# Value projections and the last projection by token, with 512 weight columns a product

## The chip, the cores and the metric

The kernel runs on one core of a Trainium2 chip. The metric is the device time of one execution in microseconds. Its time before is 1223.8 us, the median of three runs (1220.79 to 1223.92).

## The reference

Two blocks of a transformer-like network follow each other on 256 tokens of width 1024, in float32. The parts that the change touches are the value projections and the last projection:

```python
# first block, layer 0: retention mixer
a_val, a_gate, q, k, v, g = jnp.split(h @ w_in, splits, axis=-1)
# second block
(gq, gk, gv, gg, ga1, fq, fk, fv, ff, mq, bg) = jnp.split(h @ w_in[l], IN_OFFSETS, axis=-1)
mk, mv = jnp.split(_rmsnorm_2(mem, g_mem[l]) @ w_mem_kv[l], 2, axis=-1)
x = x + merged @ w_out[l]
h2 = _rmsnorm_2(x, g_ffn[l])
x = x + (jax.nn.silu(h2 @ w_ffn_gate[l]) * (h2 @ w_ffn_up[l])) @ w_ffn_down[l]
```

The values v, gv, fv and mv have 512 columns each. The last projection has 2816 rows of weights and 1024 columns.

## The kernel before

The residual x lies in SBUF by channel: 128 partitions, 8 blocks of 128 channels, 256 tokens (`x`, 128 x 8 x 256). Every operand of a dense product is split into a high and a low part of type F32R, and `mm3` (lines 319 to 321) adds three products: high x high, high x low and low x high. Weights come in pieces of 1 MB or less: `load` sends them over SP's queue into one of four buffers, `split` makes the high part on ACT (L314) and the low part on DVE (L315), four chunks a piece, into one of two buffers.

`lin` takes 128 x 128 blocks of the weights as the stationary operand and 256 tokens of the activation as the moving one; its result lies by channel. `lin_tok` does the reverse for the values, which are wanted by token: 128 x 128 blocks of the activation are stationary, and 256 columns of the weights move. A value projection is two pieces of 256 columns, in the mixer of the first block (L567), for the memory (`tok` at L1238), and twice in the second block (gv at L1347, fv at L1430). Their results go to two PSUM banks of the tag "mm"; ACT copies them out, scaled per token in `tok`.

`memory` is a generator whose steps are put between other work: one for the norm, one for each half of the keys, one for each half of the values. `memat` (1, 3, 0) says how many are taken behind the S5 layer, how many ahead of the second feed-forward stage, and how many behind it; what is left is drained behind it (L1676, L1677).

The last stage is `swiglu` (L1517). `up(q)` makes the hidden activations of part q, of 4, 4 and 3 pairs of weight pieces (L1539 to L1542 on DVE, L1540 on ACT); `down(q)` multiplies them by their rows of `w_down` into four PSUM banks of the tag "at", by channel, with `lin`. The order is up(0), up(1), down(0), up(2), down(1), down(2). In the last `down`, each bank's result is scaled per token (L1552), added to x (L1553) and sent out by channel.

The order of instructions on each engine, and on SP's queue, is not the order of the source. A planner puts it down once, from its own estimates of durations and from the order in which the source states the work: of what is ready, the earlier stated goes first. Each queue then runs strictly in that order, so a transfer that waits holds everything behind it on SP.

Of the kernel before, what the change touches and what calls it, by code (L numbers as in the profile page):

```python
# [7 lines left out]
F32 = mybir.dt.float32  # L8
# [3 lines left out]
AF = mybir.ActivationFunctionType  # L12
ALU = mybir.AluOpType
MT = bass.MemoryType
T = 256
# [14 lines left out]
def layout(v):  # L30
# [41 lines left out]
    d["w_down"] = dense(f(v["w_ffn_down_2"])[0])  # L72
# [102 lines left out]
class K:  # L175
# [155 lines left out]
    def lin_tok(self, ps, W, act):  # L331

        for k in range(8):
            for c in range(2):
                s = slice(c * 128, c * 128 + 128)
                self.mm3(ps[:, c], act[0][:, k, s], act[1][:, k, s], W[0][:, k], W[1][:, k],
                         k == 0 and c == 0, k == 7 and c == 1)
# [163 lines left out]
    def mixer0(self, x, h, fill, need, after_conv, each):  # L501
        nc = self.nc
# [62 lines left out]
        for j in range(2):  # L565
            ps = self.pair()
            self.lin_tok(ps, step_piece("w_in", 8 + j), h)  # L567
            nc.scalar.copy(v[:, :, 256 * j:256 * j + 256], ps)
# [595 lines left out]
    def tok(self, dst, name, js, h, rc):  # L1164

        for n, j in enumerate(js):
            ps = self.pair()
            self.lin_tok(ps, self.piece(name, j), h)
            for b in range(2):
                self.nc.scalar.activation(dst[:, b, 256 * n:256 * n + 256], ps[:, b], AF.Copy, scale=rc[:, b:b + 1])  # L1170
# [49 lines left out]
    def memory(self):  # L1220
# [16 lines left out]
        for n in range(2):  # L1237
            self.tok(self.mv[:, :, 256 * n:256 * n + 256], "w_mkv", (2 + n,), (hh, hl), rc)  # L1238
            yield
# [29 lines left out]
    def block2(self, x, h, rc, rb, each):  # L1269
# [77 lines left out]
        self.tok(gv, "w_in2", (2, 3), h, rc)  # L1347
# [82 lines left out]
        self.tok(fv, "w_in2", (10, 11), h, rc)  # L1430
# [86 lines left out]
    def swiglu(self, x, h, rb):  # L1517
# [4 lines left out]
        acc = [self.pair("at") for _ in range(4)]  # L1522
        hid = {}
        parts = ((0, 4), (4, 4), (8, 3))
        bc = rb[:, None, :].to_broadcast([128, 2, T])
        rh = self.keep([128, T], "rh")
        v.tensor_scalar_mul(rh, rb, 0.5)
        bch = rh[:, None, :].to_broadcast([128, 2, T])
# [16 lines left out]
        def down(q):  # L1545
            j0, nj = parts[q]
            for j in range(4):
                self.lin(acc[j], self.piece("w_down", j, 2 * j0, 2 * nj), hid[q], [(k, k) for k in range(2 * nj)], start=q == 0, stop=q == 2)
                if q == 2:
                    s = slice(2 * j, 2 * j + 2)  # L1550
# [6 lines left out]
        for q in range(3):  # L1557
            if q < 2:
                up(q + 1)
            down(q)  # L1560
# [156 lines left out]
```

## Time and profile before

| | us |
|---|---|
| median of three runs | 1223.8 |
| lowest and highest | 1220.79, 1223.92 |
| the profiled execution | 1223.6 |
| its span, first to last instruction | 1221.8 |

| engine | busy us | share of the span |
|---|---|---|
| PE (products) | 1164.1 | 95% |
| DVE | 888.7 | 73% |
| ACT | 610.9 | 50% |
| POOL | 96.8 | 8% |

The profile is one execution. A product's record lasts from its start to the end of its last column, and products overlap, so the distance from start to start is what counts. The DMA engines move 219 GB/s on average. The granted clock is TensorE's, as a share of 2.4 GHz; it is 0.979 over the span.

### The profile page before, as it was taken

How to read it: one execution, taken by the hardware profiler on the slowest of the kernel's cores; microseconds unless marked ns; L12 is line 12 of the kernel's file. 1: busy time of each engine (PE TensorE's matmuls, PEld its weight loads, DVE VectorE, ACT ScalarE, POOL GpSimd, SP SyncE). 2: the span in 40 equal slices, each digit the busy share in tenths (PEclk: the TensorE clock that was granted, in tenths of full speed). 3: DMA queues.
4: the chain of work that ended last, by engine and by line, in shares of the span. 5: the costliest groups of instructions: out<-in, count | busy, mean ns of one | idle time of the engine just before them, and what ended most of it. 6: DMA issues, size and time to landing. Idle time of an engine off the chain costs nothing. (4 is left out here: it accounts for less than half of the span.)

```text
span 1221.8 us, 25406 instructions
## 1 busy us (share of the span) xinstructions
PE 1164.1 (95%) x10482; PEld 1106.0 (91%) x10482; DVE 888.7 (73%) x1827; ACT 610.9 (50%) x1202; POOL 96.8 (8%) x132
## 2 busy tenths in 40 slices
PE   5899898999999966899999999999999999999998
PEld 3698688999999954899999999999999999999998
DVE  7879988988988869757666556676666676665564
ACT  3577345555555441646444445563465535544441
POOL 0077310000000015000000000000000000000000
PEclk9799998999999988999999999999999999999999
DMA  9888785688987999554565654452444454555541
GB/s 343 326 317 322 293 325 200 229 311 267 323 299 261 300 254 319 193 175 167 197 224 208 219 196 165 153 189 74 173 139 142 170 173 157 189 173 181 195 152 61
DMA packets 69979, 267.29 MB, mean 219 GB/s; under 512 B 7380, under 2 KB 35428, under 8 KB 43240
## 3 DMA queue, kind: packets, MB, share of 16 engines
q1 hardware_dynamic: 69864, 265.68, 63.4%
q8 instruction: 82, 1.34, 0.4%
q14 instruction: 33, 0.27, 0.1%
HBM read 246.85 MB, written 18.81 MB: 217 GB/s over the span
## 5 line engine op out<-in xcount | busy, mean ns | idle before, releaser
L315 DVE TENSOR_TENSOR lo<-w,hi 128x512 fp32r<-128x512 f32 (+1 forms) x640 | 422.5, 704 | 145.1 <-ACT hi L314 144.6
L314 ACT ACTIVATE hi<-w 128x512 fp32r<-128x512 f32 (+1 forms) x640 | 358.0, 625 | 325.4 <-PE mm L320 123.3
L319 PE MATMUL mm<-h,hi 128*128 128x256 f32 x1328 | 382.4, 288 | 1.3 <-ACT hi L314 0.8
L321 PE MATMUL mm<-h,lo 128*128 128x256 f32 x1328 | 380.4, 287 | 0.1
L320 PE MATMUL mm<-h,hi 128*128 128x256 f32 x1328 | 379.7, 286 | 0.2 <-DVE h L384 0.2
L319 PEld LDWEIGHTS mm<-h,hi 128*128 128x128 f32 x1328 | 257.0, 194 | 9.1 <-issue 3.6
L321 PEld LDWEIGHTS mm<-h,lo 128*128 128x128 f32 x1328 | 256.9, 194 | 2.7 <-issue 1.3
L320 PEld LDWEIGHTS mm<-h,hi 128*128 128x128 f32 x1328 | 256.9, 194 | 1.3 <-issue 0.7
L320 PE MATMUL at<-s,hi 128*128 128x256 f32 x720 | 204.4, 284 | 0.0
L319 PE MATMUL at<-s,hi 128*128 128x256 f32 x720 | 204.4, 284 | 0.0
L321 PE MATMUL at<-s,lo 128*128 128x256 f32 x720 | 203.9, 284 | 0.0
L319 PEld LDWEIGHTS at<-s,hi 128*128 128x128 f32 x720 | 138.0, 192 | 1.8 <-issue 1.4
L320 PEld LDWEIGHTS at<-s,hi 128*128 128x128 f32 x720 | 138.0, 192 | 0.6 <-issue 0.6
L321 PEld LDWEIGHTS at<-s,lo 128*128 128x128 f32 x720 | 137.8, 192 | 0.4 <-issue 0.4
L443 PE MATMUL fa<-wa,crep 128*32 128x256 f32 x704 | 52.9, 418 | 7.7 <-DMA wa<-in_ada_dram 3.5
L541 POOL TENSOR_TENSOR s<-s,cv 128x256 f32<-128x256 f32 x60 | 50.1, 872 | 39.5 <-ACT cv L540 39.4
L443 PEld LDWEIGHTS fa<-wa,crep 128*32 128x32 f32 x704 | 20.8, 116 | 26.8 <-DMA wa<-in_ada_dram 5.4
L319 PE MATMUL fp<-h,hi 128*128 128x256 f32 x144 | 41.1, 286 | 1.5 <-ACT hi L314 1.5
L320 PE MATMUL fp<-h,hi 128*128 128x256 f32 x144 | 40.9, 284 | 0.0
L321 PE MATMUL fp<-h,lo 128*128 128x256 f32 x144 | 40.7, 283 | 0.0
L540 ACT ACTIVATE cv<-ap,s 128x256 f32<-128x256 f32 x60 | 29.5, 506 | 17.3 <-POOL s L541 16.5
L937 ACT COPY Wt<-fp 128x512 f32<-128x512 f32 x32 | 18.6, 582 | 35.2 <-PE fp L936 28.5
(438 smaller groups left out, 1809.7 us busy)
## 6 DMA issues: line engine op xcount, KB each, us to landing
w<-in_fc_dram SPq DMA_DIRECT2D x64, 1024.0 KB, 5.0
wa<-in_ada_dram SPq DMA_DIRECT2D x44, 1024.0 KB, 6.1
w<-in_w_in_dram SPq DMA_DIRECT2D x38, 1024.0 KB, 4.9
w<-in_w_gate_dram SPq DMA_DIRECT2D x11, 1024.0 KB, 4.9
w<-in_w_up_dram SPq DMA_DIRECT2D x11, 1024.0 KB, 4.8
Vd<-V SPq DMA_DIRECT2D x16, 512.0 KB, 5.5
w<-in_w_out_dram SPq DMA_DIRECT2D x8, 1024.0 KB, 5.5
Wd<-Wt SPq DMA_DIRECT2D x16, 512.0 KB, 6.0
```

What stands on the lines that cost most here:

```text
L314: self.nc.scalar.activation(hi, h, AF.Copy)
L315: self.nc.vector.tensor_tensor(lo, h, hi.bitcast(F32), op=ALU.subtract)
L319: mm(ps, sh, mh, start=start, stop=False, skip_group_check=True)
L320: mm(ps, sh, ml, start=False, stop=False, skip_group_check=True)
L321: mm(ps, sl, mh, start=False, stop=stop, skip_group_check=True)
L443: nc.tensor.matmul(ps[32 * q:32 * q + 32], self.crep[:, 2 * k + k2], w[:, n:n + 256], start=k == 0 and k2 == 0, stop=k == 3 and k2 == 1, t ...
L540: nc.scalar.mul(t, src, w)
L541: nc.gpsimd.tensor_tensor(acc[:, ch], acc[:, ch], t, op=ALU.add)
L937: nc.scalar.copy(W[:, :, k], pt.rearrange("p (e x) -> p e x", e=4))
```

## The change

The value projections and the last projection get weights laid out in pieces of 512 columns (`w_v`, which holds the four value weights one after another, and `w_down`). `lin_tok` now multiplies 512 moving columns at once, for one half of the tokens and then the other, into two whole PSUM banks of the tag "at". A piece holds 4 row blocks by 512 columns in place of 8 by 256. `tok` evicts 512 columns at once. The memory's two value steps become one.

In `swiglu` the last projection's result now lies by token. For the sum the residual is wanted by token too: `turned` turns each of its eight blocks in squares of 32 on DVE (`v.transpose`), and 32 transfers on SP's queue put the squares where they belong; it is stated behind up(0). The final scaling and addition are one operation on DVE, in place, and the output leaves by token: four transfers of 256 KB, as before. The scale per token is kept as a column (`rt`) in place of a row (`rh`). In the last part the pieces of `w_down` have 4 and 2 row blocks.

```diff
--- before.py
+++ after.py
@@ -69,7 +69,9 @@
     d["w_out2"] = dense(f(v["w_out_2"])[0])
     d["w_gate"] = dense(f(v["w_ffn_gate_2"])[0])
     d["w_up"] = dense(f(v["w_ffn_up_2"])[0])
-    d["w_down"] = dense(f(v["w_ffn_down_2"])[0])
+    d["w_down"] = dense(f(v["w_ffn_down_2"])[0], 512)
+    w2v = lambda a: w2[:, a:a + 512]
+    d["w_v"] = con(np.concatenate([dense(a, 512) for a in (f(v["w_in"])[0][:, 2048:2560], w2v(512), w2v(2576), f(v["w_mem_kv_2"])[0][:, 512:])]))
 
     gp = lambda a: f(a)[0].reshape(2, 4, 16, 64).transpose(0, 3, 2, 1).reshape(128, 64)
     d["lam_re"], d["lam_im"] = con(gp(v["s5_lam_re"])), con(gp(v["s5_lam_im"]))
@@ -328,13 +330,20 @@
                 self.mm3(ps[:, ci], W[0][:, k, s], W[1][:, k, s], act[0][:, ka], act[1][:, ka],
                          start and n == 0 and ci == 0, stop and n == len(ks) - 1 and ci == len(cols) - 1)
 
-    def lin_tok(self, ps, W, act):
-
-        for k in range(8):
-            for c in range(2):
-                s = slice(c * 128, c * 128 + 128)
-                self.mm3(ps[:, c], act[0][:, k, s], act[1][:, k, s], W[0][:, k], W[1][:, k],
-                         k == 0 and c == 0, k == 7 and c == 1)
+    def lin_tok(self, ps, W, act, ks, start, stop):
+
+        for b in range(2):
+            s = slice(b * 128, b * 128 + 128)
+            for n, (k, ka) in enumerate(ks):
+                self.mm3(ps[b], act[0][:, ka, s], act[1][:, ka, s], W[0][:, k], W[1][:, k],
+                         start and n == 0, stop and n == len(ks) - 1)
+
+    def values(self, i, act, piece=None):
+
+        ps = [self.ps("at") for _ in range(2)]
+        for k0 in (0, 4):
+            self.lin_tok(ps, (piece or self.piece)("w_v", i, k0, 4, 512), act, [(k, k0 + k) for k in range(4)], k0 == 0, k0 == 4)
+        return ps
 
 
     def rsqrt(self, v, out=None):
@@ -562,10 +571,8 @@
             qk.append(dst)
         q, k = qk
         v = self.sb([128, 2, 512])
-        for j in range(2):
-            ps = self.pair()
-            self.lin_tok(ps, step_piece("w_in", 8 + j), h)
-            nc.scalar.copy(v[:, :, 256 * j:256 * j + 256], ps)
+        for b, ps in enumerate(self.values(0, h, step_piece)):
+            nc.scalar.copy(v[:, b], ps)
         rh, rl, ah, al = (self.sb([128, 4, T], F32R) for _ in range(4))
         os, ms = [], []
         for j in range(2):
@@ -1161,13 +1168,10 @@
         return u
 
 
-    def tok(self, dst, name, js, h, rc):
-
-        for n, j in enumerate(js):
-            ps = self.pair()
-            self.lin_tok(ps, self.piece(name, j), h)
-            for b in range(2):
-                self.nc.scalar.activation(dst[:, b, 256 * n:256 * n + 256], ps[:, b], AF.Copy, scale=rc[:, b:b + 1])
+    def tok(self, dst, i, h, rc):
+
+        for b, ps in enumerate(self.values(i, h)):
+            self.nc.scalar.activation(dst[:, b], ps, AF.Copy, scale=rc[:, b:b + 1])
 
     def heads(self, dst, name, js, h, g, rc, out=None):
 
@@ -1234,9 +1238,8 @@
         for n in range(2):
             self.heads(self.mk[:, 2 * n:2 * n + 2], "w_mkv", (n,), (hh, hl), self.col("g_mem_k"), rc)
             yield
-        for n in range(2):
-            self.tok(self.mv[:, :, 256 * n:256 * n + 256], "w_mkv", (2 + n,), (hh, hl), rc)
-            yield
+        self.tok(self.mv, 3, (hh, hl), rc)
+        yield
 
     def norm2_begin(self, x):
 
@@ -1344,7 +1347,7 @@
         self.mark("b2.gla")
 
         gv = self.sb([128, 2, 512])
-        self.tok(gv, "w_in2", (2, 3), h, rc)
+        self.tok(gv, 1, h, rc)
         gs = self.sb([128, 4, T])
         for c in range(2):
             pg = self.pair()
@@ -1427,7 +1430,7 @@
                     v.scalar_tensor_tensor(A[:, hd, o:o + nk], pn[:, 256 * a:256 * a + nk], cq[:, b, hd:hd + 1], causal[:, T - nk:], op0=ALU.add, op1=ALU.add)
         self.heads(fq, "w_in2", (6, 7), h, gq[:, 0:1], rc, rq[:, 0:4])
         self.heads(fk, "w_in2", (8, 9), h, self.col("g_fox_k"), rc)
-        self.tok(fv, "w_in2", (10, 11), h, rc)
+        self.tok(fv, 2, h, rc)
 
         def fox(hd, po):
             pl = self.ps()
@@ -1514,18 +1517,26 @@
             v.scalar_tensor_tensor(x[:, 2 * j:2 * j + 2], ps, 0.5, x[:, 2 * j:2 * j + 2], op0=ALU.mult, op1=ALU.add)
             each(j)
 
-    def swiglu(self, x, h, rb):
+    def swiglu(self, x, h, rb, rt):
 
         nc, v = self.nc, self.nc.vector
         tt = v.tensor_tensor
         K8 = [(k, k) for k in range(8)]
-        acc = [self.pair("at") for _ in range(4)]
         hid = {}
         parts = ((0, 4), (4, 4), (8, 3))
+        acc = [[self.ps("at") for _ in range(2)] for _ in range(2)]
+
+        xt, xb = self.sb([128, 2, 1024], tag="xt"), self.sb([128, 8, T], tag="xt")
+
+        def turned():
+            for k in range(8):
+                v.transpose(xb[:, k], x[:, k])
+            for i in range(4):
+                for j in range(4):
+                    for b in range(2):
+                        nc.sync.dma_start(xt[32 * j:32 * j + 32, b].rearrange("p (k i s) -> p k i s", k=8, i=4)[:, :, i],
+                                          xb[32 * i:32 * i + 32, :, 128 * b + 32 * j:128 * b + 32 * j + 32])
         bc = rb[:, None, :].to_broadcast([128, 2, T])
-        rh = self.keep([128, T], "rh")
-        v.tensor_scalar_mul(rh, rb, 0.5)
-        bch = rh[:, None, :].to_broadcast([128, 2, T])
 
         def up(q):
             j0, nj = parts[q]
@@ -1544,16 +1555,19 @@
 
         def down(q):
             j0, nj = parts[q]
-            for j in range(4):
-                self.lin(acc[j], self.piece("w_down", j, 2 * j0, 2 * nj), hid[q], [(k, k) for k in range(2 * nj)], start=q == 0, stop=q == 2)
+            for m in range(2):
+                for k0 in range(0, 2 * nj, 4):
+                    kn = min(4, 2 * nj - k0)
+                    self.lin_tok(acc[m], self.piece("w_down", m, 2 * j0 + k0, kn, 512), hid[q], [(k, k0 + k) for k in range(kn)],
+                                 q == 0 and k0 == 0, q == 2 and k0 + kn == 2 * nj)
                 if q == 2:
-                    s = slice(2 * j, 2 * j + 2)
-                    t = self.sb([128, 2, T])
-                    tt(t, acc[j], bch, op=ALU.mult)
-                    tt(x[:, s], t, x[:, s], op=ALU.add)
-                    nc.sync.dma_start(self.out[:, s], x[:, s])
+                    for b in range(2):
+                        o = xt[:, b, 512 * m:512 * m + 512]
+                        v.scalar_tensor_tensor(o, acc[m][b], rt[:, b:b + 1], o, op0=ALU.mult, op1=ALU.add)
+                        nc.sync.dma_start(self.out[:, b, 512 * m:512 * m + 512], o)
 
         up(0)
+        turned()
         for q in range(3):
             if q < 2:
                 up(q + 1)
@@ -1692,12 +1706,15 @@
 
                 self.block2(x, made[0][0], rc, rb, each)
             mem_pools.close()
-            with self.phase(s8=4):
+            with self.phase(s8=4, xt=2):
                 self.mark("norm2f")
                 rb = self.keep([128, T], "rb2")
-                nc.scalar.copy(rb, self.rms(x, st))
+                r = self.rsqrt_eps(self.sumsq(x, st)[:, :, 0])
+                nc.scalar.copy(rb, self.spread(r))
+                rt = self.keep([128, 2], "rt")
+                nc.vector.tensor_scalar_mul(rt, r, 0.5)
                 self.mark("swiglu")
-                self.swiglu(x, out[0][0], rb)
+                self.swiglu(x, out[0][0], rb, rt)
 
 
 def kernel(**inputs):
@@ -1708,9 +1725,9 @@
     nc = bacc.Bacc("TRN2", target_bir_lowering=False, num_devices=1)
     arrays = {f"in_{n}_dram": a for n, a in layout(inputs).items()}
     I = {n[3:-5]: nc.dram_tensor(n, a.shape, mybir.dt.from_np(a.dtype), kind="ExternalInput").ap() for n, a in arrays.items()}
-    out = nc.dram_tensor("out_0_dram", (128, 8, T), F32, kind="ExternalOutput").ap()
+    out = nc.dram_tensor("out_0_dram", (128, 2, 1024), F32, kind="ExternalOutput").ap()
     with tile.TileContext(nc, schedule_with_timeline_sim=True) as tc:
         K(tc, I, out, None).build()
     r = run_bass_kernel_spmd(nc, [arrays], core_ids=[0])
     got = r.results[0]["out_0_dram"]
-    return np.ascontiguousarray(got.transpose(2, 1, 0).reshape(1, T, 1024))
+    return np.ascontiguousarray(got.transpose(1, 0, 2).reshape(1, T, 1024))
```

## Rows read from the trace of the kernel before

**Rows 1.** The page, part 1: PE's busy time, share of the span, instructions.

```profile
PE 1164.1 (95%) x10482; PEld 1106.0 (91%) x10482; DVE 888.7 (73%) x1827; ACT 610.9 (50%) x1202; POOL 96.8 (8%) x132
```

**Rows 2.** By stage: busy us (count) PE PEld DVE ACT POOL, clock, DMA.

```profile
100.00:200.00 100.00, 92.90 (x865) 79.05 (x864) 89.14 (x197) 49.49 (x103) 34.85 (x34) 0.97 0.82 301
430.00:500.00 70.00, 44.17 (x738) 34.10 (x738) 54.99 (x104) 26.54 (x47) 24.71 (x38) 0.81 0.95 269
500.00:762.00 262.00, 262.00 (x2193) 261.95 (x2192) 167.71 (x328) 132.39 (x251) 2.87 (x3) 1.00 0.56 197
762.00:1024.00 262.00, 262.00 (x2118) 256.88 (x2116) 180.79 (x432) 138.14 (x281) 0.00 (x0) 0.99 0.45 152
1024.00:1177.00 153.00, 152.71 (x1271) 152.31 (x1271) 96.16 (x168) 72.37 (x136) 0.00 (x0) 1.00 0.53 178
```

**Rows 3.** Timeline of PE in the last projection: start us, us, line, tiles, shape.

```profile
1192.53 0.28 PE L320 MATMUL at<-s,hi 128*128 128x256 f32 x1
1192.65 0.28 PE L321 MATMUL at<-s,lo 128*128 128x256 f32 x1
```

**Rows 4.** Stretch around 45 us: its granted clock, and PE's timeline there.

```profile
44.00:47.00 3.00, 3.00 (x16) 3.00 (x16) 3.00 (x7) 1.31 (x3) 0.00 (x0) 0.50 0.87 311
44.20 0.41 PE L319 MATMUL mm<-h,hi 128*128 128x256 f32 x1
...
45.27 0.41 PE L321 MATMUL mm<-h,lo 128*128 128x256 f32 x1
```

**Rows 5.** PE's timeline near 763 and 940 us, and L1486 by form.

```profile
763.26 0.95 PE L167 MATMUL fa<-nw,q 128*128 128x2 f32 x8
...
764.27 0.28 PE L320 MATMUL mm<-lo,mhh 128*128 128x256 f32 x1
...
768.27 0.28 PE L321 MATMUL mm<-hi,mhl 128*128 128x256 f32 x1
...
939.74 1.02 PE L1486 MATMUL at<-s,mv 128*128 128x256 f32 x4
L1486 PE MATMUL at<-s,mv 128*128 128x256 f32 x16 | 4.1, 378 | 0.0
```

**Rows 6.** Groups by form: line, engine, operation, shape, count, busy us, mean ns.

```profile
L448 DVE STREAM_TRANSPOSE s<-fa 128x256 f32<-128x256 f32 x11 | 4.9, 444 | 0.1
L315 DVE TENSOR_TENSOR lo<-w,hi 128x512 fp32r<-128x512 f32 x632 | 414.1, 699 | 137.0 <-ACT hi L314 136.5
L1170 ACT ACTIVATE s<-mm,rc 128x256 f32<-128x256 f32 x8 | 3.4, 473 | 8.7 <-PE mm L321 8.1 <-DVE rc L1261 0.6
```

**Rows 7.** Weight loads: SP's queue, time to landing, and ACT's first reads.

```profile
1093.49 17.61 SPq L298 DMA_DIRECT2D w<-in_w_down_dram  x4
...
w<-in_w_down_dram SPq DMA_DIRECT2D x8, 1024.0 KB, 4.8
...
1113.34 2.19 ACT L314 ACTIVATE hi<-w 128x512 fp32r<-128x512 f32 x4 [3.04 <-issue]
```

**Rows 8.** SP's queue: transfers of small runs.

```profile
237.60 0.43 SPq L925 DMA_DIRECT2D Kd<-Ks  x1
238.07 0.43 SPq L924 DMA_DIRECT2D Kd<-Ks  x1
...
466.58 13.53 SPq L1027 DMA_DIRECT2D Mt<-Kd  x8
```

**Rows 9.** Timeline of the end: PE and DVE.

```profile
1216.77 0.28 PE L321 MATMUL at<-s,lo 128*128 128x256 f32 x1
1217.09 0.69 DVE L1552 TENSOR_TENSOR s<-at,rh 128x512 f32<-128x512 f32 x1 [2.90 <-PE at L321]
1217.81 0.69 DVE L1553 TENSOR_TENSOR x<-s,x 128x512 f32<-128x512 f32 x1
```

**Rows 10.** ACT and DVE behind the second feed-forward stage.

```profile
764.00 0.62 ACT L155 ACTIVATE q<-x 128x512 f32<-128x512 f32 x1
...
769.37 0.16 DVE L354 TENSOR_SCALAR s<-fa 128x2 f32<-128x2 f32 x1 [4.29 <-PE fa L167]
```

## The prediction

> **What bounds the kernel now.** I read the busy times and clock of the page first, then the table by stage, then the timeline of TensorE, and last the queue of weight loads. The page has PE busy 95% of the span [rows 1], and busy alone says little, since one product is recorded with 0.28 us while the next starts 0.12 us later. The table by stage [rows 2] says where it matters: from 500 us to the end PE is busy in every microsecond at a granted clock of 0.99 to 1.00, while DVE has 63 to 69% of those stages and ACT about half. In that part the end moves with the sum of the starts of PE's products. Before 500 us it is not so: from 430 to 500 us PE has 44 of 70 us, and from 100 to 200 us DVE has 89%.
>
> The unit of that sum is the pitch, the time from one start to the next. In the last projection one product starts at 1192.53 and the next at 1192.65, 120 ns [rows 3], and so it goes on to the last. I measured what it is made of at three other places. Around 45 us the granted clock is 0.50, the level of 1.2 GHz, and five starts of the same product take 1.07 us, 214 ns each [rows 4]: that is 256 periods of 1.2 GHz (213), one column a period, and nothing on top. At full clock 256 periods are 107 ns, so the 120 hold 13 ns that are not columns. Second, eight products with two moving columns and new weights for each, followed by the next one, take from 763.26 to 764.27, 1.01 us for nine: 112 ns with almost no column to stream [rows 5]. So a load of 128 weight columns alone sets a floor of that size. Third, the memory's values start 34 times from 764.27 to 768.27, 117.6 ns each [rows 5], with the same shape as the others. A rate of streaming would give the same number at every place. I read the 120 as a floor of the weight load, not of the 256 columns.
>
> What a product costs that keeps the array about 512 periods behind its own weight load is seen at L1486: plain float32, 256 columns, new weights each. Four of them are busy 1.02 us, of which the last one's record is 0.378: three starts in 0.64 us, 214 ns [rows 5]. 512 periods of 2.4 GHz are 213 ns. The load vanishes under them.
>
> **The change part by part.** *Fewer, wider products.* The code gives the counts. A value projection has 8 row blocks by 2 token halves by 2 column pieces by 3 products of 256 columns, 96; after it 48 of 512. There are four places: the mixer, the memory, and two of block 2. The last projection has 22 row blocks by 8 by 3, 528, and 264 after. I price a new product at 216 ns, L1486's pitch and a little, because that row is nearest: as many array periods, as many weight columns. The bounds are 213 (columns alone) and 240 (two of today's). A pair at 120 gives back 240 - 216 = 24 ns; one of the memory's gives back 235 - 216 = 19.
> - Two value places of block 2: 2 x 48 x 24 ns = 2.3 us. Memory: 48 x 19 = 0.9 us. All on a full PE.
> - Last projection: 264 x 24 = 6.3 us, on a full PE.
> - Mixer: 48 x 24 = 1.15 us, in the stage where DVE has 89%. From nothing to all of it; I take 0.6.
>
> The Trainium skill (TensorE: Matmul & The Clock Gate, Back-to-back issue gap) gives the gap of an isolated product at full clock as its columns at 2.4 GHz plus 2.5 ns. By it 256 columns should start every 109 ns and 512 every 216, and a pair would be worth 2.5 ns. The rows agree with it on the long product and not on the short one, and it is the short one that the change removes.
>
> *The end.* The last product starts at 1216.77; two DVE operations of 0.69 us follow, then the transfer [rows 9]. After the change one fused operation does both, and the other half of that column piece has ended 12 products earlier. That is 0.7 us off the end. The transfer stays at 256 KB.
>
> *Turning the residual.* Eight transposes of 128x256. The same operation takes 0.444 us at L448 [rows 6], so 3.6 us of DVE; four additions of 0.69 us and the scaled row go. DVE is free for a third of that stage [rows 2], and the result is wanted only some 100 us later, at the first column piece's end. One transpose in front of a weight split holds it up by 0.44 us, and the splits are made a piece ahead. I take nothing, and 1 us as the upper bound.
>
> Then 32 transfers on SP's queue, each of 32 KB in 256 runs of 128 B. The weight loads of the stage go through the same queue, and each of the 32 waits, at the head of it, for the transposes. What covers them is the slack of the loads: the one issued at 1093.49 lands in 4.8 us and is first read at 1113.34, so 15 us are to spare, and loads follow each other by 5.8 us [rows 7]. No row has this transfer. By its bytes the nearest are the 28 and 32 KB ones of a few SBUF rows, issued every 0.47 us [rows 8]: 32 x 0.47 = 15 us, which the slack just covers. By its number of runs the nearest are the eight to Mt, 13.53 us for eight, 1.69 each [rows 8]: 54 us. I take 0.5 us each, because those eight carry four times the bytes, read device memory and wait for each other's landing. That is 16 us, and since the first load that is held falls due somewhere inside them, a stall of 0 to 1 us; I take 0.5.
>
> *Moved work.* The memory's generator had one step for each half of its values; the third step before the second feed-forward stage ran the first half, and the rest was drained behind it. Now the third step runs both. So 48 products leave the place behind that stage, where they stand from 761.88 to 768.27, and their successors join a place in front of it that is full anyway. What they covered: the last square of the residual begins on ACT at 764.00, and the inverse root on DVE at 769.37 [rows 10]. The products next in line are 24 of the small projection, 18 of which don't need the last chunk (2.2 us), and the first value piece, whose results stay in two "at" banks until the root is there. Between 761.9 and 765.1 that leaves 1.0 us uncovered, 3.2 if nothing is pulled forward, nothing if the value piece fills it. I take 0.5. The root itself can start some 3 us earlier.
>
> *Small things at nothing.* Evictions of values become two of 512 columns in place of four of 0.473 us [rows 6], on ACT, hidden under the next products. Load bytes and the number of weight pieces stay. The order inside a piece (all blocks of one token half first) asks for the four split chunks within 2.6 us instead of 5.8; a chunk takes DVE 0.70 us [rows 6], and splitting starts a piece ahead. If DVE were late by one operation, it would cost 0.7 us at each such piece.
>
> *Sum.* Gains 2.3 + 0.9 + 6.3 + 0.6 + 0.7 = 10.8; costs 0.5 + 0.5 = 1.0; net 9.8. The profiled execution took 1223.6 us (span 1221.8 and 1.8 around it), which is the median of the three runs, 1223.8, less 0.2. 1223.6 - 9.8 = 1213.8 us. With the small costs at their bounds, 1210 to 1218.
>
> **The rivals.** *The 13 ns belong to each product.* If switching weights under a full-rate stream costs it that time whatever its length, a new one has 227 ns and a pair gives 13 (memory 8): 1.3 + 0.4 + 3.5 + 0.3 + 0.7 - 1.0 = 5.2, so 1218.4. For it: L1486 streams at half the columns a period, so a clash of two full-rate reads would not show there; the 112 ns of almost empty products are below 120. Against it: the half clock shows none of it.
>
> *The 13 ns belong to the columns.* Then 512 cost 240 and only the end and the costs are left: 1223.9. The rule of the Trainium skill named above (TensorE: Matmul & The Clock Gate, Back-to-back issue gap), with 2.5 ns a pair, would give 1222.8, 1.1 us less than this case. Against it: 117.6 ns over 34 starts.
>
> *The turned squares choke SP's queue, slower than before.* If the 32 stand in one block and take T, the load held behind them is late by T less the 15 us of slack and, on average, half a load interval of 2.9. At 1.0 us each, T is 32 and PE waits 14 us: 1228; at Mt's 1.69 it is 1250. It decides from a stall of 10 us on, T = 28, 0.88 us a transfer. For it: 256 runs each, and Mt's rows. Against it: a quarter of the bytes, and a planner that may put loads between them. The Trainium skill (DMA: Bandwidth & Descriptors, Why small descriptors are slow (HBM only)) says that transfers between SBUF places do not pay the penalty of small runs. No row here has such a transfer to test it.
>
> **How the numbers follow.** Forecast 0.56, product-bound extra 0.21, column-bound 0.09, choked queue 0.10; 0.04 for a rearranged plan in the first 500 us that does something else. About 0.3% (3.7 us) is what a measurement here can tell from no change, so faster means below 1220.1: the forecast, nearly all of the first rival (0.18) and a little of the rest, 0.75. Within: 0.14, most of it the column case. Slower: 0.11, mainly the queue. The range runs from 1209 (the forecast's low end, less 1 us for a better plan) to 1225, past the column case; it leaves out the queue, the unnamed case and little else.
>
> **What would show it.** The pitch of the 512-column products in TensorE's timeline: 216, 227 or 240 ns decides among the first three. The turn: 32 issues on SP, their spacing, and whether weight splits on ACT wait for a DMA within 60 us of them. A gap on PE behind the second feed-forward stage shows the moved cover. One DVE operation between the last product and the last transfer. The prediction is wrong if PE has waits of several us after 1030 us, or if the part before 500 us differs by more than 2 us.

## The result, and the profile of the kernel after

The changed kernel takes 1259.2 us (median of 4 runs, 1256.9 to 1260.3) against 1222.3 for the kernel before on the same chip: a ratio of 1.030, 95% interval 1.0285 to 1.0321. It is 37 us slower. The forecast was 1213.8, 10 us faster.

The page of the kernel after, part 1, to be held against [rows 1]:

```profile
PE 1172.9 (93%) x10026; PEld 1090.9 (87%) x10026; DVE 891.1 (71%) x1837; ACT 610.5 (49%) x1202; POOL 96.9 (8%) x132
```

PE (TensorE) has 456 instructions fewer and 9 us more of busy time; the other engines do what they did. By stage, with the columns of [rows 2]:

```profile
100.00:200.00 100.00, 88.80 (x793) 72.36 (x792) 82.85 (x177) 45.74 (x95) 34.84 (x34) 0.98 0.76 283
500.00:762.00 262.00, 246.10 (x1991) 241.81 (x1983) 157.14 (x314) 124.76 (x235) 1.91 (x3) 0.95 0.50 182
762.00:1024.00 262.00, 252.52 (x1911) 241.68 (x1910) 171.99 (x419) 135.39 (x272) 2.87 (x3) 0.96 0.41 144
1024.00:1177.00 153.00, 152.75 (x1200) 149.16 (x1199) 103.79 (x185) 72.97 (x137) 0.00 (x0) 1.00 0.57 186
```

In [rows 2] the two stretches of 262 us had PE full. Now 15.9 and 9.5 us of them are empty, and the granted clock is 0.95 and 0.96. The last stretch is full as before. So the loss isn't in the last projection; PE waits in the middle of the kernel. Where it waits is seen from the start of the same instruction in both traces. A "spread" in this table and below is the small product that brings one number per token (a root) onto all partitions:

| first start of | before, us | after, us | later by | change of it |
|---|---|---|---|---|
| the first product of the stage behind the state space part | 498.4 | 507.3 | 9.0 | +9.0 |
| the small projection of block 2 | 769.2 | 793.9 | 24.7 | +15.7 |
| the last norm's spread | 1036.9 | 1076.4 | 39.5 | +14.8 |
| the last product | 1216.8 | 1252.7 | 35.9 | -3.6 |
| the end | 1221.8 | 1257.2 | 35.4 | -0.5 |

Three places lose 9, 16 and 15 us, and the last projection and the end give back 4.1. PE's timeline of the kernel after at the second place (start us, us, line, tiles, shape, idle before it and what ended that):

```profile
573.75 0.95 PE L1205 MATMUL at<-inv,q 128*128 128x1 f32 x8
585.41 2.07 PE L378 MATMUL at<-ident,s 128*128 128x128 f32 x8 [10.71 <-DVE s L1194]
587.27 1.71 PE L1205 MATMUL at<-inv,q 128*128 128x1 f32 x8
591.90 2.05 PE L378 MATMUL at<-ident,s 128*128 128x128 f32 x8 [2.92 <-DVE s L1194]
593.60 0.77 PE L321 MATMUL at<-hi,mhh 128*128 128x512 f32 x1
594.17 0.63 PE L322 MATMUL at<-lo,mhh 128*128 128x512 f32 x1
594.60 0.63 PE L323 MATMUL at<-hi,mhl 128*128 128x512 f32 x1
```

and at the third:

```profile
798.97 0.28 PE L323 MATMUL at<-h,lo 128*128 128x256 f32 x1
805.62 1.22 PE L378 MATMUL fp<-ident,rc 128*128 128x128 f32 x4 [6.37 <-DVE rc L1264]
807.30 1.23 PE L378 MATMUL fp<-ident,s 128*128 128x128 f32 x4 [0.46 <-ACT rb L1266]
808.45 1.22 PE L1322 MATMUL at<-s,s 16*128 16x256 f32 x2
810.24 1.22 PE L1322 MATMUL at<-s,s 16*128 16x256 f32 x2 [0.56 <-ACT l L1323]
813.22 0.37 PE L1342 MATMUL at<-ident,s 4*128 4x4 f32 x2 [1.77 <-DVE s L1339]
813.52 0.80 PE L321 MATMUL at<-hi,h 128*128 128x512 f32 x1
```

In both, the value products (`at<-hi`) come after a string of small products: spreads of a root (`at` at the second place, `fp` at the third), squares of heads, the products of the small projection's chain. Most of these wait for VectorE, and PE waits with them. Before, PE had products to run there, and no wait. At the second place the memory's value products stood on both sides of the first group's squares, products of the next stage (`mm<-h`) followed, and they ran until the group's spread could start:

```profile
566.23 0.95 PE L1201 MATMUL at<-inv,q 128*128 128x1 f32 x8
567.04 0.36 PE L320 MATMUL mm<-lo,mhh 128*128 128x256 f32 x1
...
571.25 0.28 PE L319 MATMUL mm<-h,hi 128*128 128x256 f32 x1
...
585.50 1.05 PE L369 MATMUL at<-ident,s 128*128 128x128 f32 x8
```

At the third place 94 of them ran from 772.15 to 783.31, while the root was made:

```profile
772.15 0.28 PE L319 MATMUL mm<-hi,h 128*128 128x256 f32 x1
...
783.31 0.28 PE L319 MATMUL mm<-hi,h 128*128 128x256 f32 x1
783.43 0.60 PE L369 MATMUL fp<-ident,rc 128*128 128x128 f32 x4
```

And the output tile has another name: the memory's values are `mm<-hi,mhl` in [rows 5] and `at<-hi,mhl` here. `at` is a ring of four result banks, `mm` one of two: tiles of a tag get its banks in turn. The change took the values' banks from `at`.

And in the kernel after PE gets no other work while the values stand back. By the code there are two buffers for split weights, and the values' two pieces hold both until their products have run. ACT's timeline bears it out: at the second place it splits no weights between these two lines, and the second starts just behind the last of the 24 products of the values' first piece (recorded until 600.55). At the third place it is the same, from 801.4 to 821.3 us. So the products of the next stage are held up too.

```profile
575.50 1.14 ACT L316 ACTIVATE hi<-w 128x512 fp32r<-128x512 f32 x2
...
600.63 2.19 ACT L316 ACTIVATE hi<-w 128x512 fp32r<-128x512 f32 x4 [20.80 <-issue]
```

The wait has a second price: the products behind it start every 0.43 us, 512 periods of 1.2 GHz, at a granted clock of 0.50 (593.6 to 596 us, and 813.6 to 817.5), until the clock is back at 1.00.

The pitch of the long product in the last projection, where [rows 3] had 0.12 us:

```profile
1216.62 0.39 PE L323 MATMUL at<-hi,s 128*128 128x512 f32 x1
...
1217.30 0.39 PE L323 MATMUL at<-hi,s 128*128 128x512 f32 x1
```

Three products later it is 0.68 us later, 227 ns a product; 384 starts of such products at full clock, those of three value places among them, have a mean of 227.3. That is neither the forecast's 216 nor 240. The end, against [rows 9]:

```profile
1252.66 0.39 PE L323 MATMUL at<-hi,s 128*128 128x512 f32 x1
1253.09 0.75 DVE L1566 SCALAR_TENSOR_TENSOR xt<-at,rt,xt 128x512 f32<-128x512 f32 x1 [0.38 <-PE at L323]
```

One VectorE operation is left there, and from the last product to the end it is 4.5 us where it was 5.0.

### The profile page after: what moved, and what is told of

Same layout as the page of the kernel before. It is cut to its first block, busy times and chain, and to the rows that moved or that the text cites. A ratio compares the mean times of both kernels' runs of the same rounds, so it can differ in the third digit from the quotient of the medians.

```text
span 1257.2 us, 24528 instructions
## 1 busy us (share of the span) xinstructions
PE 1172.9 (93%) x10026; PEld 1090.9 (87%) x10026; DVE 891.1 (71%) x1837; ACT 610.5 (49%) x1202; POOL 96.9 (8%) x132
## 4 chain that ended last, share of the span: by engine, by line
PE 57%; DVE 2%; ACT 1%; POOL 0%; issue 0%; ACTq 0%; POOLq 0%
PE mm L322 10%; PE mm L321 10%; PE mm L323 10%; PE at L321 5%; PE at L322 5%; PE at L323 5%; PE fp L321 1%; PE fp L322 1%; PE fp L323 1%; PE fa L323 1%; PE fa L322 1%; PE fa L321 1%; PE fp L378 1%; PE at L169 1%; PE at L378 1%; PE fa L1205 0%
## 5 line engine op out<-in xcount | busy, mean ns | idle before, releaser
L317 DVE TENSOR_TENSOR lo<-w,hi 128x512 fp32r<-128x512 f32 x646 | 422.4, 699 | 162.1 <-ACT hi L316 161.3
L316 ACT ACTIVATE hi<-w 128x512 fp32r<-128x512 f32 x646 | 358.5, 620 | 348.4 <-issue 129.6
L321 PE MATMUL at<-s,hi 128*128 128x256 f32 x544 | 155.9, 287 | 0.0
L322 PE MATMUL at<-s,hi 128*128 128x256 f32 x544 | 155.0, 285 | 0.0
L323 PE MATMUL at<-s,lo 128*128 128x256 f32 x544 | 154.6, 285 | 0.0
L321 PEld LDWEIGHTS at<-s,hi 128*128 128x128 f32 x544 | 104.9, 193 | 2.2 <-issue 1.8
L323 PEld LDWEIGHTS at<-s,lo 128*128 128x128 f32 x544 | 104.6, 193 | 0.8 <-issue 0.8
L322 PEld LDWEIGHTS at<-s,hi 128*128 128x128 f32 x544 | 104.9, 193 | 0.4 <-issue 0.4
```

What stands on the lines that cost most here:

```text
L316: self.nc.scalar.activation(hi, h, AF.Copy)
L317: self.nc.vector.tensor_tensor(lo, h, hi.bitcast(F32), op=ALU.subtract)
L321: mm(ps, sh, mh, start=start, stop=False, skip_group_check=True)
L322: mm(ps, sh, ml, start=False, stop=False, skip_group_check=True)
L323: mm(ps, sl, mh, start=False, stop=stop, skip_group_check=True)
```

## The experiments

Theory: the values' results joined the ring of four, which the serial chains use (a chain is a row of small operations that wait for each other, such as a norm's root), so their products can no longer run while a chain runs. Rivals: the shape (512 columns, halves of tokens, row pieces) throws the order whatever the bank; the memory's moved step bares the root behind the second feed-forward stage; the last projection's transfers cost. The runs of the kernel before lay between 1219 and 1228 us in these experiments, with a standard deviation of 2 us, so where a kernel has a single time and no interval, it is good to some 4 us. Differences are taken against the kernel before on the same chip.

### Each half of the change alone

The last projection's part alone (weight pieces, `swiglu`, the transposes and transfers, the output by token; all value places as before), then the values alone:

```
-    d["w_down"] = dense(f(v["w_ffn_down_2"])[0])
+    d["w_down"] = dense(f(v["w_ffn_down_2"])[0], 512)
...
```

> The kernel before with the last projection's part of the change alone: 512 weight columns by token, the turned residual with its 32 transfers, the result by token. All four value places and the memory's steps stay as they were. Theory (the whole loss is in the value places, and a 512-column product has 227 ns): 264 products of 227 ns in place of 528 of 120 give back 3.5 us, one vector operation fewer at the end some 0.5 us, so 1222.3 - 4.0 = 1218. Rival one (216 ns a product, as forecast): 1222.3 - 7 = 1215. Rival two (the 32 transfers hold up the weight loads): 1226 or more, with waits of TensorE for weights within 60 us of the transfers.

Measured: 1217.7 against 1221.8, ratio 0.9967, interval 0.9954 to 0.9979. The sum with 227 ns a product holds. This kernel is 4.1 us faster than the one before and the fastest of all that were run. From 500 us to 1212 PE has one wait, of 0.2 us, and the turned squares go out in four groups of 7, 8, 7 and 10 with a weight load behind each (SP's queue: start, time that the issues took, line, tiles, count):

```profile
1022.79 4.85 SPq L1556 DMA_DIRECT2D xt<-xt  x7
1027.76 0.52 SPq L300 DMA_DIRECT2D w<-in_w_up_dram  x1
...
1040.63 7.03 SPq L1556 DMA_DIRECT2D xt<-xt  x10
```

> The kernel after with the last projection as before (256 columns, by feature, no turned residual): only the four value places and the memory's single step are changed. Theory (all of the loss lies here): 1259.2 + 4 = 1263. If part of the loss came with the last projection, its transfers or the re-made plan of the whole, it is below 1255.

Measured: 1263.9, 42 more than before, a single run. All of the loss is in the values.

### One place at a time

From the kernel before, one of the four value places changed as in the kernel after (512 columns, ring of four; the memory's also in one step).

> The kernel before with one value place changed, the mixer's: 512 columns, two banks from the ring of four. Everything else as before. Theory now (the mixer loses by itself, in the stage where VectorE is near full): 8 to 11 us slower than before, 1230 to 1233, all of it there by 210 us. Rival (the loss before 500 us came with the re-made plan of the whole program): within 3 us of before.

Measured: 1234.6, 12.7 more than before, a single run.

> The kernel before with one value place changed, the memory's: 512 columns, one step, two banks from the ring of four. Theory (the ring): the values come behind the root of the norm and the two head groups, whose spreads and squares stand in the same ring, and PE waits 14 us there, as at 574 and 588 us of the kernel after; with the 2 us that the moved step cost by itself 1236 to 1240. If 512 columns by themselves or the moved step were all: 1221 to 1225.

Measured: 1243.6, 21.2 more, a single run, above what the theory gave. The longest of PE's waits from 540 to 830 us, where the kernel before has none (what waited, for what: us, times, longest):

```profile
PE at L386 <- DVE s L1212: 13.6, 2, 10.7
PE fp L386 <- DVE rc L1282: 1.5, 1, 1.5
```

> The kernel before with one value place changed, the first of block 2: 512 columns, its two banks from the ring of four. The memory's values stay in two steps, so 48 products still stand behind the second feed-forward stage. Theory (the ring): the values come behind the norm's root, the small projection and its chain; 10 to 15 us lost there, 1232 to 1238. Rival two (the moved memory step): its cover is in place, so 1221 to 1224.

Measured: 1232.9, 11 more, a single run, with the wait at the third place as in the kernel after although the memory's second step was in its old place:

```profile
PE fp L386 <- DVE rc L1283: 6.2, 1, 6.2
PE at L1361 <- DVE s L1358: 1.8, 1, 1.8
```

> The last value place of block 2 alone by 512 columns, its banks from the ring of four. No root stands behind it: 48 products at 13 ns a pair, 0.6 us less than before, so 1220 to 1223. If the ring costs here too: 1228 or more.

Measured: ratio 0.9991, interval 0.9969 to 1.0014. The same ring and the same products, and no loss. The code has a reason: in block 2 the squares and spreads of the heads in front of these values use other banks (`fa` and `fp`), so no link of theirs stands in that ring.

The four places and the last projection add up to 12.7 + 21.2 + 11.1 - 0.9 - 4.1 = 40; measured were 37. Within the noise of three single runs the places are independent, so each is looked at by itself.

### The ring of four against the ring of two

The tag from which the two result tiles come is changed, from "at" to "mm" (the same at the other three places):

```
-        ps = [self.ps("at") for _ in range(2)]
+        ps = [self.ps(tag) for _ in range(2)]
...
-        self.tok(self.mv, 3, (hh, hl), rc)
+        self.tok(self.mv, 3, (hh, hl), rc, "mm")
```

First in all four places:

> The kernel after with one word changed: the two result banks of each value projection come from the ring of two banks that the other projections use, not from the ring of four that the roots, spreads, head squares and the small projection use. Shapes, weights, order of loops and the memory's single step stay as in the kernel after. Theory (the ring decides: values that stand behind the chains' own results in the ring of four can't run while the chains do): the products stand in front of the chains again, and the waits of 11 and 3.3 us near 574 and 6.7 us and more near 799 go; 39 us of the loss less a few for the small ring, 1219 to 1228. Rival one (the wide pieces or the order of token halves cost the time, whatever the bank): 1255 or more. Rival two (the memory's step that was moved left the root behind the feed-forward stage bare): the wait of 6 us behind that stage stays, 1235 to 1245.

Measured: 1234.4, ratio 1.0115, interval 1.0071 to 1.0159. Some 25 of the 37 us come back, fewer than the theory said. The waits at the second place are gone but for one of 0.3 us. Two losses stay: 10 us before 509 us, and at the third place one wait:

```profile
PE fp L378 <- DVE rc L1264: 4.3, 1, 4.3
```

Then place by place:

> As the run of the memory's place alone, but the two result banks come from the ring of two. Theory (the ring): no wait at the head groups; what is left is the moved step's 2 us less half a microsecond of the wider products: 1222 to 1225. If the width or the order of token halves causes the wait: 1235 or more.

Measured: 1228.9 against 1243.6 with the ring of four. The waits of 13.6 us have gone, and the longest that is left is the same as there:

```profile
PE fp L386 <- DVE rc L1282: 1.5, 1, 1.5
```

So 14.7 us of the memory's place are the ring's, between two single runs. It is still 4 above the expected 1225, which a single time doesn't tell from noise.

> The first value place of block 2 alone by 512 columns, as in the run that gave 1232.9, but with its two banks from the ring of two. Theory (the ring of four): its products stand in front of the root again, 1221 to 1225; what is left above before is the wait of 3.6 us for a split that the run with both places of block 2 showed. If the width or the halves cost the 11 us: 1230 or more.

Measured: 1227.1, ratio 1.0044, interval 1.0023 to 1.0065; with the ring of four it was 1232.9. Over the kernel before that is 4 to 5 us against 11, so some 6 to 7 us are the ring's. Of the 4 to 5 that stay, most is the only wait that PE has there:

```profile
PE mm L321 <- DVE l L1381: 3.3, 1, 3.3
```

L1381 is not a split, as the expectation had it; it reads and so empties a bank of the ring of two, and it stands on VectorE behind operations of the small projection's chain. So the ring of two has its own price, as the code and this wait are read: the values hold both banks until the root scales them, the other projections, which fill the chain's time, come later, and a product waits for a bank that is emptied behind the chain.

> Down part as in the kernel after; of the values only the two places of block 2 by 512 columns, with their result banks from the ring of two; mixer and memory as before. Theory: the last projection alone gave 4.1 us; two places of 48 products at 13 ns a pair give 1.3 more, since both hold the same two banks as before: 1216.4. Rival (a value place by token holds both banks to its end and the work of the other projections waits): 1219 to 1224.

Measured: 1220.7, ratio 0.9992, interval 0.9977 to 1.0007. The theory falls here: the two places of block 2 should have added 1.3 us to the 4.1 of the last projection, and took some 3 of them away; the same wait of 3.3 us is in the trace. So even in the better ring the value places of block 2 aren't worth having by 512 columns.

### The memory's step

The kernel before with only the two yields merged into one:

```
         for n in range(2):
             self.tok(self.mv[:, :, 256 * n:256 * n + 256], "w_mkv", (2 + n,), (hh, hl), rc)
-            yield
+        yield
```

> The kernel before with one thing changed: the memory's generator runs both halves of its values in one step, as in the kernel after; products, banks and shapes stay. 48 products of 118 ns then no longer stand behind the second feed-forward stage. The recorded step had 0.5 us for it, 0 to 3.2. Theory from the trace with the small ring (a wait of 4.7 us behind that stage): 4 to 7 us slower, 1226 to 1229. If the planner covers the root with other work: within 1.5 us.

Measured: ratio 1.0013, interval 1.0003 to 1.0023: 1.6 us, with one wait of 1.5 us for the root and one of 0.8. The theory of 4 to 7 fails, and the recorded bounds of 0 to 3.2 us hold. The moved step alone is not the loss.

### The mixer

> The kernel before with the mixer's values alone by 512 columns, their two banks from the ring of two. If the ring of four cost the 12.7 us of the mixer's place: within 3 us of before. If it is the wide products, the order of token halves or the row pieces, or a plan that falls out otherwise: 1230 or more, as the run of all places with the ring of two showed a loss of 10 us there.

Measured: 1234.0, a single run. The mixer's loss doesn't depend on the ring. So what is it? The copies first:

> The kernel before with the products of the mixer's values untouched (256 columns, same banks, same order), but the two copies of the results put behind both of them, so that no head's values are there before the last product, as with 512 columns by token half. Theory one (the first heads start late because their values are whole only at the end): 6 to 11 us slower, 1228 to 1233. Theory two (width, ring or plan): within 3 us of before.

Measured: 1220.8, a single run. It isn't that the first heads get their values late. Then the order of the products inside a piece, against the kernel with the mixer's values alone in the ring of four:

```
-        for b in range(2):
-            s = slice(b * 128, b * 128 + 128)
-            for n, (k, ka) in enumerate(ks):
+        for n, (k, ka) in enumerate(ks):
+            for b in range(2):
+                s = slice(b * 128, b * 128 + 128)
...
```

> The mixer's values alone by 512 columns, as in the run of that place with the ring of four, but within a piece both token halves of one row block follow each other, so that a split chunk is asked for every 1.4 us as before the change. If the bursts of chunks (all four in 2.7 us) cost the mixer's 12 us: within 3 us of before. If not: 1230 or more.

Measured: 1233.1, ratio 1.0081, interval 1.0061 to 1.0101. The bursts of chunks aren't it. Then the width, with 256 columns in the new pieces:

> The kernel before with the mixer's values by token halves from row pieces of 512 columns and into banks of the ring of four, as in the kernel after, but each product again 256 columns wide: 96 of them, and 5.7 us for each piece as before. If the width (the time of a product, 227 ns for one in place of two of 120) throws the mixer's order: within 3 us of before. If banks, pieces or the order of halves do: 1230 or more.

Measured: 1228.6, a single run. Neither answer: about half of the loss is left when the width is taken back.

The trace of the kernel before and that of the ring of two agree up to 145 us, within 1 us. There a root for the second group of heads begins on VectorE, and behind it the group's spread, the mean and the variance of the convolution, the last root and the output projection follow in one row. First and last operation of that root in the kernel before, and PE's spread:

```profile
145.30 0.16 DVE L354 TENSOR_SCALAR s<-at 128x4 f32<-128x4 f32 x1
...
149.71 0.16 DVE L349 SCALAR_TENSOR_TENSOR s<-s,s 128x4 f32<-128x4 f32 x1
149.93 1.16 PE L369 MATMUL at<-ident,s 128*128 128x128 f32 x8 [0.59 <-DVE s L349]
```

and in the kernel with the mixer's values alone by 512 columns (ring of two):

```profile
145.10 0.16 DVE L371 TENSOR_SCALAR s<-at 128x4 f32<-128x4 f32 x1 [0.33 <-PE at L1221]
...
148.53 1.29 DVE L317 TENSOR_TENSOR lo<-w,hi 128x512 fp32r<-128x512 f32 x2
...
149.80 1.29 DVE L317 TENSOR_TENSOR lo<-w,hi 128x512 fp32r<-128x512 f32 x2
...
152.27 0.16 DVE L366 SCALAR_TENSOR_TENSOR s<-s,s 128x4 f32<-128x4 f32 x1
157.39 1.05 PE L386 MATMUL at<-ident,s 128*128 128x128 f32 x8
```

Four splits of an output piece stand inside the root (the piece's load was issued at 140.81, before at 143.91). The root takes 7.3 us in place of 4.6, and then PE takes the first output products ahead of the spread, which comes 7.5 us late. The changed kernel, with the ring of four, shows the same on a smaller scale: four splits stand inside that root, it takes 6.8 us, and its spread starts at 154.35, 4.4 us late. The experiment, with the ring of two, adds one order: the splits of the first two output pieces stand behind `root`, VectorE's last operation of that root.

```
-            return piece(*a)
+            with self.held_at(getattr(self, "root", {})):
+                return piece(*a)
...
+        DVE = mybir.EngineType.DVE
+        root = {DVE: self.last(DVE)}
...
```

> The mixer's values alone by 512 columns, ring of two, and one order added on VectorE: the splits of the output projection's first two pieces stand behind the root of the second head group, which in the run without this order took 7.3 us among them in place of 4.6. Theory (the splits in front of the root start the loss; the mean, the variance and the last root follow it in a row): 3 to 8 us less than the 1234 of that run, 1226 to 1231. If the root is not on the path: 1233 or more.

Measured: 1226.3, ratio 1.0029, interval 1.0006 to 1.0052. Over the kernel before that is 3.4 us, where it was 11.6 without the order, so it gives back some 8 us; and the spread is within 1 us of where it was:

```profile
150.43 0.16 DVE L366 SCALAR_TENSOR_TENSOR s<-s,s 128x4 f32<-128x4 f32 x1
150.65 1.16 PE L386 MATMUL at<-ident,s 128*128 128x128 f32 x8 [1.18 <-DVE s L366]
```

The loads of that piece are as early here (141.62), so it was the order and not the load. So two thirds of the mixer's loss in the ring of two are an order on VectorE and PE that came out worse. In the ring of four, which the changed kernel has, that order was not tried, and the rest of the loss was not found. Why the planner chose the worse order, when the values' last product starts 0.5 us earlier than before (113.89 against 114.41), is not settled; neither the halves, nor the late copies, nor the ring alone brings it about.

### The transfers of the turned residual

The kernel with the last projection's part alone, its transposes and transfers twice:

```
         up(0)
         turned()
+        turned()
```

> The kernel with the last projection's part alone, its eight transposes and 32 transfers issued twice. In that kernel the 32 go out in four groups between the weight loads, 0.6 to 0.75 us each, 23 us in all. If they are hidden: 46 us still fit between loads that are needed only every 5.8 us, 1217 to 1219, no waits of TensorE for weights. If SP's queue is what they are paid in: the second 32 hold up the loads by 10 us or more, 1225 or above.

Measured: 1226.4, ratio 1.0029, interval 1.0009 to 1.0050, against 1217.7 for the same kernel with one turn on another chip. Each against the kernel before on its own chip, they are 3.0 us slower and 4.1 us faster, 7.1 apart. The first 32 went out in four groups as above. The second 32 stand in one block, and PE waits once for a split behind it. SP's queue:

```profile
1053.01 21.46 SPq L1556 DMA_DIRECT2D xt<-xt  x32
1074.57 0.54 SPq L300 DMA_DIRECT2D w<-in_w_up_dram  x1
1075.21 0.38 SPq L300 DMA_DIRECT2D w<-in_w_gate_dram  x1
```

The wait, from PE's waits between 1070 and 1090 us:

```profile
PE fa L321 <- ACT hi L316: 4.1, 1, 4.1
```

A transfer in a block costs 21.46 / 32 = 0.67 us. The block is longer than the cover, PE waits 4.4 us from start to start, and the products after it run at half clock (granted clock 0.50 from 1079 to 1083 us) and lose another 2.6 us: 7.0 of the 7.1 us. One turn alone went out in four groups with loads between them and was hidden; what it would cost in one block was not run.

## Why the prediction was wrong

*What bounds the kernel: right, and not followed to its end.* PE was full from 500 us on, so the end moved with the sum of its starts and with every wait that came in. The prediction added up the starts. It looked for new waits in two places, SP's queue and the root behind the second feed-forward stage, and not in the banks.

*The step that failed* stands in "Moved work". The memory's products "join a place in front of it that is full anyway", at no price, and "the first value piece, whose results stay in two 'at' banks until the root is there" is counted as work that could be pulled forward into the root's time. The runs show 21.2 us lost at the first of these places and 11 at the second. The prediction saw the new banks and read them as room. But between the second feed-forward stage and the values the code asks the same ring for three banks: for the small projection, for its chain's two products and for the transposed sums. The values' two are the fourth and fifth request of a ring of four, so one of them has to wait for a bank that is free only when the root has been applied to what it holds. In the trace the values came behind all three; which request held them back is not shown, but that the ring did is, by the change of tag alone. The same holds for the memory, behind the squares and spreads of its two groups of heads. The tag alone decided 14.7 us at the memory, some 6 to 7 at the first place of block 2, and some 25 of the 37 in all. A rule that speaks for the change stands in the Trainium skill (Perfetto Trace Analysis, Matmuls): groups of products should rotate through different banks, and larger products are more efficient. Here both were done; the last projection gained 4.1 us, of which the longer products make 3.5 by their pitch, and the rotation put work that could have run behind work that had to wait.

*The pitch: the mechanism was read wrongly, the rival was right.* The step was "I read the 120 as a floor of the weight load". Long products measure 227 ns, 213 and 14 more, as the first rival had it: an extra of 13 to 14 ns is there at either length. So a pair gives 13 ns and not 24, and the last projection 3.5 us and not 6.3. The row that misled is the plain float32 of [rows 5]: it takes 214 ns for 256 columns, two periods a column, and shows no extra; the rival had said that such a row wouldn't show one. With 256 columns it isn't a long product either, so the sentence that the rows agree with the page's rule "on the long product" had no row behind it. That rule of the Trainium skill is for an isolated product (TensorE: Matmul & The Clock Gate, Back-to-back issue gap), 2.5 ns above its columns; by it a pair would give 2.5 ns, and the trace has 13.

*The memory's price a pair* was taken as 235 - 216 = 19. Its long products start every 233.1 ns (41 starts), and two short ones took 235: 2 ns. The other places have 227 and 120. This difference wasn't explained before and isn't now.

*The end:* 0.7 us forecast, 0.5 measured.

*Turning the residual:* eight transposes, 0.42 us each, hidden, as said. A transfer was taken at 0.5 us, bounds 0.47 and 1.69; it is 0.67 in a block. The slower rival's sum, T less the 15 us of slack and 2.9 of half a load interval, gives 21.5 - 17.9 = 3.6 us for one block, and the doubled turn measured 4.4. With one turn the planner put loads between the transfers, which the prediction had named as its counter-argument. The Trainium skill (DMA: Bandwidth & Descriptors, Why small descriptors are slow (HBM only)) says that moves inside SBUF are spared the penalty of small runs. Whether that holds here no run shows: 0.67 us is more than the 0.47 us of the 28 and 32 KB transfers of a few rows, and less than Mt's 1.69 [rows 8], which carry four times the bytes.

*The moved step:* 0.5 us, bounds 0 to 3.2; by itself 1.6 us. Inside the bounds. It grows when the root's other cover goes too: with all values in the ring of two the wait for the root was 4.3 us and not 1.5.

*The mixer:* "From nothing to all of it; I take 0.6", a gain of 1.15 at most. This was the second step that failed. The place lost 12.7 us. In a stage with VectorE at 89% [rows 2] and a chain through it, a bound of zero from below was not justified: in the ring of two the order of splits and root alone moved the end by some 8 us. The prediction gave 0.04 to "a rearranged plan in the first 500 us".

*What would show it:* the signs were well chosen. The part before 500 us does differ by more than 2 us, and there is a gap behind the second feed-forward stage. After 1030 us there is no wait above 0.2 us, so the last stage was the part that was understood.

## What to carry to other kernels

A new result bank from a ring is a place in that ring's queue. Before a filler's tiles are moved to another ring, list who asks that ring between the filler and the work that it covers; if a chain's own links are among them, expect the filler to run after the chain, and count what else is held up meanwhile: here the filler's weights kept both split buffers. And cost a change in a full stage not by the work alone but by who stands in front of whom: where a planner makes the order, leave the bound open on the losing side, also where the sum says gain.

## What the runs showed of the hardware that was not expected

The extra of 13 to 14 ns a product is the same under 256 columns (120 ns) and 512 (227 ns) at full clock, and absent at half clock, where 512 columns start every 0.43 us, just as [rows 4] had it for 256. The memory's values are an exception with 118 and 233 ns.

A wait of PE costs more than its length. After 4.4 us of it, in the run with two turns, the next products of 256 columns started every 0.21 us in place of 0.12, at a granted clock of 0.50, until 2.6 us were lost on top; in the kernel after, products of 512 columns behind the waits started every 0.43 us in place of 0.23.

A transfer of 32 KB between SBUF places in 256 runs of 128 B takes 0.67 us of SP's queue when 32 of them follow each other.
